# Convolution module of a two-layer trunk: GpSimd's additions moved to VectorE and TensorE

## The chip, the cores and the metric

The kernel runs on one core of a Trainium2 chip. The metric is the device time of one execution in microseconds (us). The engines are named as the profile names them: PE is TensorE (PEld its weight load), DVE is VectorE, ACT is ScalarE, POOL is GpSimd, SP is the engine whose queue issues most transfers.

## The reference, cut to what matters

Two layers run over 512 tokens of width 1024. Layer 0 is attention, layer 1 is the convolution module below, and each is followed by an expert mixer that takes most of the time. All of it is fp32.

```python
def conformer_conv(h, w_pw1, b_pw1, w_dw, b_dw, g_ln, b_ln, w_pw2, b_pw2):
    d = h.shape[-1]
    a = h @ w_pw1 + b_pw1
    a = a[..., :d] * jax.nn.sigmoid(a[..., d:])
    a = lax.conv_general_dilated(a, w_dw[:, None, :], ..., feature_group_count=d) + b_dw   # 31 taps per channel
    a = jax.nn.silu(layer_norm(a, g_ln, b_ln))
    return a @ w_pw2 + b_pw2

y_lat = conformer_conv(a_lat, *conv_p)
h_lat = h_lat + g1[:, None, :] * y_lat
```

## The kernel before

Channels lie on the 128 partitions, so the 1024 channels are eight blocks (f = 0 to 7), and the 512 tokens lie along the free axis. Nothing is scheduled by a planner here: every engine runs its instructions in the order in which `conv` issues them, and waits for a tile of another engine by semaphore.

An fp32 product is made of three matmuls on a high and a low half of each operand (`matmul3`, profile lines L142, L143, L144). The halves of a weight tile are made by `split`: ACT copies the high half (`cu_hi`, L1624), POOL subtracts it for the low half (`cu_lo`, L1625).

For every block `glu(f)` does two products of 24 matmuls each (`pw1`, weights `cu_raw` streamed by SP into two buffers, split two products ahead), a sigmoid on ACT (`sg`, L1664) and a multiplication on DVE that writes the padded block `pad` (L1668). Then the 31 taps of the block are run by one of four ways, by the letter in `CONV_BY = "vvgpvvmp"`:

- v: 31 instructions on DVE (`conv_dve`; L1680 and L1682 are its first two, L1684 all others, L1686 the sum of its two accumulators);
- g: ACT scales the shifted block (`tap`, L1698) and POOL adds it up (L1699), in `conv_pool`;
- m: 16 taps on DVE, 15 by ACT and POOL, added at L1779;
- p: on PE, 31 taps of three matmuls on diagonal matrices (`conv_pe`). The diagonals are built by one DVE instruction for the high half (`build_diag`, L1707) and 31 ACT instructions for the low half (L1710), and `split_pad` halves the block (L1717, L1718).

The lists `vq`, `gq` and `dq` hold the taps that are due, and `advance` issues so many of them after each `glu`. Then comes the layer norm: the mean by PE (`mu`, L1740), the subtraction (L1792), the variance by PE (`var`, L1795), a reciprocal square root on POOL, and per block a scaling on DVE (`xn`, L1815), a SiLU and a copy on ACT (`xs`, `sT`) and the low half of `sT` on DVE (L1823). Beside it POOL multiplies the last bias by the gate (L1803) and adds it to the residual `h` (L1805, four times).

The last product is a `RowProduct`: eight rows of weights `wo_raw` are loaded, multiplied by the gate on POOL (`prescale`, L1537) and split (`wo_hi` on ACT L1549, `wo_lo` L1550 on POOL for the first two rows and on DVE after that). `run` goes through the rows one after the other with 24 matmuls each (L1567), and adds the result to `h` at the end. `norm_transposed` ahead of all this transposes and modulates the input; its low halves (`caT`, L132) go to DVE and POOL in turn.

Of the kernel before, what the change touches and what calls it, by code (L numbers as in the profile page):

```python
# [25 lines left out]
T = 512  # L26
TT = 4
# [87 lines left out]
        return [self.out[tt] for tt in range(TT)]  # L115


def norm_transposed(k, work, ps, xr, A, sh, hi, lo, per_k=None):

    nc = k.nc  # L120
    nt = TT
    fs = {}
    for kk in range(KD + 2):
        if kk < KD:
            p = ps.tile([128, nt, 128], F32, name="nt_p", bufs=2)
            for tt in range(nt):
                nc.tensor.transpose(p[:, tt, :], xr[tt][:, kk * 128:(kk + 1) * 128], k.ident)
            f = work.tile([128, nt * 128], F32, name="nt_f", bufs=4)
            nc.scalar.activation(f, p.rearrange("p a b -> p (a b)"), AF.Identity, scale=A[:, kk:kk + 1],
                                 bias=sh[:, kk:kk + 1])  # L130
            nc.vector.tensor_copy(hi[:, kk, :], f)
            (nc.gpsimd if kk % 2 else nc.vector).tensor_tensor(lo[:, kk, :], f, hi[:, kk, :].bitcast(F32),  # L132
                                                               op=OP.subtract)
            fs[kk] = f
        if kk >= 2 and per_k is not None:
            per_k(kk - 2, fs.pop(kk - 2))
# [1384 lines left out]
class RowProduct:  # L1521

    BUFS = 3

    def __init__(self, k, raw_pool, src, scale):
        self.k, self.rp, self.src, self.scale, self.raw = k, raw_pool, src, scale, {}
        self.n = self.ns = 0

# [5 lines left out]

    def prescale(self):
        t = self.raw[self.ns]
        self.k.nc.gpsimd.tensor_tensor(t, t, self.scale, op=OP.mult)  # L1537
        self.ns += 1

    def split(self, j, eng=None):  # L1540
# [16 lines left out]
        for j in range(2):  # L1557
            self.split(j, eng)

    def run(self, lhs2, y, done):  # L1560
        nc = self.k.nc

        def mm(j, w2, tt):
            s = slice(tt * 128, (tt + 1) * 128)
            for n, (l, w) in enumerate(((lhs2[0], w2[0]), (lhs2[0], w2[1]), (lhs2[1], w2[0]))):
                for hf in range(2):
                    nc.tensor.matmul(y[tt][hf], lhsT=l[:, j, s], rhs=w[:, hf * 512:(hf + 1) * 512],  # L1567
                                     start=(j == 0 and n == 0), stop=(j == KD - 1 and n == 2))
        for j in range(KD - 2):
            for tt in range(TT):  # L1570
                mm(j, self.ws[j], tt)
            self.split(j + 2)
        for tt in range(TT):
            for j in (KD - 2, KD - 1):
                mm(j, self.ws[j], tt)
            done(tt)
# [2 lines left out]

CW = 31  # L1580
PADW = T + CW - 1
CONV_BY = "vvgpvvmp"
CONV_G = (6, 6, 6, 6, 6, 6, 6, 6)


def conv(k, a, h, xr, xp, hA, ada):
# [9 lines left out]
    owr = st.enter_context(k.pool("c_owr"))  # L1596
    proj = RowProduct(k, owr, lambda j: a["w_pw2"][j * 128:(j + 1) * 128, :], g1b)
    cv = cp.tile([128, KD, T], F32, name="cv")

    p1 = ExitStack()  # L1600
# [88 lines left out]
    def conv_pool(f, o, w0=0):

        pad = pads[f]
        if w0 == 0:
            S.activation(o, pad[:, 0:T], AF.Identity, scale=wdw[:, f, 0:1], bias=vec["b_dw"][:, f:f + 1])
        else:
            S.activation(o, pad[:, w0:w0 + T], AF.Copy, scale=wdw[:, f, w0:w0 + 1])
        for w in range(w0 + 1, CW):
            t = wk.tile([128, T], F32, name="tap", bufs=3)
            S.activation(t, pad[:, w:w + T], AF.Copy, scale=wdw[:, f, w:w + 1])  # L1698
            G.tensor_tensor(o, o, t, op=OP.add)  # L1699
            yield  # L1700

    diag = {}

    def build_diag(f, eng):

        d = diag[f] = [dg.tile([128, CW, 128], F32R, name="diag%d" % i) for i in range(2)]
        eng.tensor_tensor(d[0], k.ident[:, None, :].to_broadcast([128, CW, 128]),  # L1707
                          whi[:, f, :, None].bitcast(F32).to_broadcast([128, CW, 128]), op=OP.mult)
        for c in range(CW):
            S.activation(d[1][:, c, :], k.ident, AF.Copy, scale=wlo[:, f, c:c + 1])  # L1710
            yield

    def split_pad(f):
# [5 lines left out]
        return ph, pl  # L1719

    def conv_pe(f, ph, pl):
        p = ps.tile([128, T], F32, name="cz", bufs=4)
        dh, dl = diag.pop(f)
        for w in range(CW):
            matmul3(nc, p, (dh[:, w, :], dl[:, w, :]), (ph[:, w:w + T], pl[:, w:w + T]), w == 0, w == CW - 1)
        return lambda: S.activation(cv[:, f, :], p, AF.Identity, bias=vec["b_dw"][:, f:f + 1])
# [16 lines left out]
    vq, gq = [], []  # L1743
    dq = [build_diag(3, V)]
    part = wk.tile([128, T], F32, name="cv3")
    advance(dq, 8)
    for f in range(8):
        glu(f)
        by = CONV_BY[f]
        if by == "v":  # L1750
            vq.append(conv_dve(f))
        elif by == "g":
            gq.append(conv_pool(f, cv[:, f, :]))
        elif by == "m":
            vq.append(conv_dve(f, 16))
            gq.append(conv_pool(f, part, 16))
        if f == 3:
            pad_hl = split_pad(3)
        if f == 4:
            move = conv_pe(3, *pad_hl)  # L1760
        if f == 5:
            move()
            dq.append(build_diag(7, V))
            for j in range(proj.BUFS):
                proj.load()
        if f == 7:
            for g in (0, 1, 3, 2, 4):
                mean(g)
            move = conv_pe(7, *split_pad(7))
        advance(dq, 1000 if f == 6 else 12)  # L1770
        advance(vq, 26 if f == 4 else 14)
        if f == 7:
            for j in range(proj.BUFS):
                proj.prescale()
        advance(gq, CONV_G[f])
    while vq or gq:
        advance(vq, 2)
        advance(gq, 1)
    V.tensor_tensor(cv[:, 6, :], cv[:, 6, :], part, op=OP.add)  # L1779
    move()  # L1780
    us.close()
# [49 lines left out]
    def residual(tt):  # L1831
# [146 lines left out]
```

## Time and profile before

| | |
|---|---|
| median of 3 runs (lowest, highest) | 3433.71 us (3431.82, 3434.04) |
| the profiled execution: its time, its span | 3434.28 us, 3432.5 us |
| mean granted clock of PE | 0.968 |
| busy share of the span | PE 94%, PEld 81%, DVE 76%, ACT 38%, POOL 35% |
| the convolution module in the span | about 1836 to 2125 us |

The page of the profile cuts the span into 40 equal slices. The module is slices 22 to 25, which are the only ones after the start in which the PE row of tenths falls to 5 to 8, and in which the granted clock falls to 0.7 to 0.9. Times below are us from the start of the span.

### The profile page before, as it was taken

The page shows a single profiled execution, that of the slowest core. Times are in us where ns is not written, and L with a number is a line of the kernel's source. Part 1 is how long each engine was busy: PE and PEld are TensorE (multiplying, and loading weights), DVE is VectorE, ACT ScalarE, POOL GpSimd, SP SyncE. Part 2 cuts the span into 40 slices and gives each one's busy share as a digit, 9 for nine tenths or more (in the row PEclk, how much of TensorE's full clock was granted, in tenths as well). Part 3 has the DMA queues.
Part 4 walks back from the last instruction along what each step waited for, and adds up shares of the span by engine and source line. Part 5 has one row for each costly group of instructions (what it writes and reads, how often), then busy time and mean ns, then how long its engine had stood idle before and what let it go on. Part 6 is the DMA issues. An engine that isn't in the chain of part 4 may idle for free.

```text
span 3432.5 us, 46075 instructions
## 1 busy us (share of the span) xinstructions
PE 3228.5 (94%) x17044; PEld 2791.2 (81%) x17044; DVE 2604.2 (76%) x4765; ACT 1297.2 (38%) x2053; POOL 1189.0 (35%) x911
## 2 busy tenths in 40 slices
PE   8889999999999999999998757997899999999998
PEld 5766568889999999999876636887899999999986
DVE  3667646899577777777788985799777777777787
ACT  4325533344433333333334423234433333333332
POOL 1247533300133333333344844320023333333433
PEclk9989999999999999999999978998999999999999
DMA  6422224358788888889882102324788888888886
GB/s 201 153 72 72 85 99 155 105 202 294 264 301 307 303 308 303 303 302 310 312 303 88 56 13 94 121 99 183 254 284 302 304 305 311 297 308 301 305 318 213
DMA packets 373682, 764.36 MB, mean 223 GB/s; under 512 B 24144, under 2 KB 221008, under 8 KB 366160
## 3 DMA queue, kind: packets, MB, share of 16 engines
q1 hardware_dynamic: 292816, 442.62, 38.2%
q0 software_dynamic: 73728, 268.47, 22.8%
q10 hardware_dynamic: 6912, 50.33, 3.7%
q8 instruction: 133, 2.18, 0.3%
q14 instruction: 93, 0.76, 0.1%
HBM read 702.61 MB, written 58.72 MB: 222 GB/s over the span
## 4 chain that ended last, share of the span: by engine, by line
PE 73%; DVE 17%; DMA 3%; issue 3%; ACT 2%; POOL 1%; SPq 1%; ACTq 0%; DVEq 0%; POOLq 0%
PE acc L602 26%; PE s L142 11%; PE s L143 11%; PE s L144 11%; DVE cv L1684 4%; PE y L1567 2%; DVE eij L451 2%; PE ot L1352 1%; DVE al L454 1%; PE z L144 1%; DVE u_lo L173 1%; PE z L142 1%; PE z L143 1%; DVE ah L453 1%; PE scp L257 1%
## 5 line engine op out<-in xcount | busy, mean ns | idle before, releaser
L143 PE MATMUL s<-hhi,u_lo 128*128 128x384 f32 (+1 forms) x2304 | 792.8, 344 | 8.3 <-DVE u_lo L173 8.0
L142 PE MATMUL s<-hhi,u_hi 128*128 128x384 f32 (+1 forms) x2304 | 797.4, 346 | 3.0 <-ACT u_hi L169 3.0
L144 PE MATMUL s<-hlo,u_hi 128*128 128x384 f32 (+1 forms) x2304 | 791.3, 343 | 0.0
L613 POOL DMA_INDIRECT row<-in_u_dram,eidx x256 | 317.2, 1239 | 1019.3 <-DVE row L621 500.0
L613 POOL DMA_INDIRECT row<-in_v_dram,eidx x256 | 353.2, 1380 | 538.2 <-DVE gacc L625 480.1
L581 DVE TENSOR_TENSOR v_lo<-v_raw,v_hi 128x1024 fp32r<-128x1024 f32 x192 | 235.3, 1225 | 398.7 <-ACT v_hi L579 398.7
L579 ACT ACTIVATE v_hi<-v_raw 128x1024 fp32r<-128x1024 f32 x192 | 203.8, 1062 | 683.1 <-PE acc L602 646.5
L143 PEld LDWEIGHTS s<-hhi,u_lo 128*128 128x128 f32 x2304 | 436.7, 190 | 29.1 <-DVE u_lo L173 11.6
L142 PEld LDWEIGHTS s<-hhi,u_hi 128*128 128x128 f32 x2304 | 437.4, 190 | 20.0 <-ACT u_hi L169 3.7
L144 PEld LDWEIGHTS s<-hlo,u_hi 128*128 128x128 f32 x2304 | 436.4, 189 | 10.2
L602 PE MATMUL acc<-v_hi,w_hi 128*128 128x512 f32 x1344 | 418.1, 392 | 4.6 <-ACT w_hi L590 4.6
L602 PE MATMUL acc<-v_hi,w_lo 128*128 128x512 f32 x1344 | 416.3, 391 | 0.0
L602 PE MATMUL acc<-v_lo,w_hi 128*128 128x512 f32 x1344 | 416.1, 391 | 0.0
L173 DVE TENSOR_TENSOR u_lo<-u_raw,u_hi 128x1024 fp32r<-128x1024 f32 x242 | 295.0, 1219 | 45.4 <-ACT u_hi L169 45.0
L625 DVE SCALAR_TENSOR_TENSOR gacc<-row,gwgt,gacc 128x1024 f32<-128x1024 f32 x254 | 325.4, 1281 | 4.3
L169 ACT ACTIVATE u_hi<-u_raw 128x1024 fp32r<-128x1024 f32 x288 | 302.1, 1049 | 6.0 <-ACT stg L471 3.8
L621 DVE SCALAR_TENSOR_TENSOR row<-row,hg 128x1024 f32<-128x1024 f32 x256 | 300.9, 1219 | 0.0
L602 PEld LDWEIGHTS acc<-v_lo,w_hi 128*128 128x128 f32 x1344 | 252.4, 188 | 55.9
L602 PEld LDWEIGHTS acc<-v_hi,w_lo 128*128 128x128 f32 x1344 | 252.2, 188 | 54.6
L602 PEld LDWEIGHTS acc<-v_hi,w_hi 128*128 128x128 f32 x1344 | 249.1, 188 | 46.6 <-ACT w_hi L590 7.3
L590 ACT ACTIVATE w_hi<-w_f 128x384 fp32r<-128x384 f32 x256 | 134.7, 526 | 327.4 <-DVE w_f L588 306.8
L310 ACT ACTIVATE ring<-s 128x384 f32<-128x384 f32 x256 | 125.8, 491 | 323.8 <-PE s L144 323.7
(455 smaller groups left out, 5168.3 us busy)
## 6 DMA issues: line engine op xcount, KB each, us to landing
u_raw<-in_uT_dram SPq DMA_DIRECT2D x256, 512.0 KB
v_raw<-in_v_dram SPq DMA_DIRECT2D x192, 512.0 KB
Gd<-stg ACTq DMA_DIRECT2D x48, 1024.0 KB
g_in<-Gd SPq DMA_DIRECT2D x128, 384.0 KB
ada_w<-in_w_ada_dram SPq DMA_DIRECT2D x80, 512.0 KB
u_raw<-in_v_dram SPq DMA_DIRECT2D x64, 512.0 KB
u_raw<-in_wq_dram SPq DMA_DIRECT2D x32, 512.0 KB
ada_w<-in_w_ada_dram SPq DMA_DIRECT2D x8, 1024.0 KB
```

What stands on the lines that cost most here:

```text
L142: nc.tensor.matmul(out, lhsT=lh, rhs=rh, start=first, stop=False)
L143: nc.tensor.matmul(out, lhsT=ll, rhs=rh, start=False, stop=False)
L144: nc.tensor.matmul(out, lhsT=lh, rhs=rl, start=False, stop=last)
L169: nc.scalar.activation(uh, u, AF.Copy)
L173: lo_eng.tensor_tensor(ul, u, uh.bitcast(F32), op=OP.subtract)
L579: nc.scalar.activation(vh, v, AF.Copy)
L581: nc.vector.tensor_tensor(vl, v, vh.bitcast(F32), op=OP.subtract)
L602: nc.tensor.matmul(acc[tt][hf], lhsT=w[:, s], rhs=v[:, hf * 512:(hf + 1) * 512], start=f and n == 0, stop=l and n == 2)
L613: nc.gpsimd.indirect_dma_start(out=r, out_offset=None, in_=un if n < 128 else vn, in_offset=bass.IndirectOffsetOnAxis(ap=eidx[:, c:c + 1], ...
L621: nc.vector.scalar_tensor_tensor(r, r, 1.0, hg, op0=OP.mult, op1=OP.mult, accum_out=act[:, c:c + 1])
L625: nc.vector.scalar_tensor_tensor(gacc, r, wgt[:, c:c + 1], gacc, op0=OP.mult, op1=OP.add)
L1684: V.scalar_tensor_tensor(d, pad[:, w:w + T], wt, d, op0=OP.mult, op1=OP.add)
```

## The change

No arithmetic of the module is left on POOL but the reciprocal square roots of four numbers; it keeps the clearing of the 15 columns at both ends of `pad`.

- The low halves `cu_lo` and all of `caT` go to DVE.
- Blocks 0, 2, 4, 6 have all 31 taps on DVE; blocks 1, 3, 5 all 31 on PE; block 7 has 21 on PE and 10 on DVE, added at the end (before: DVE 0, 1, 4, 5; PE 3, 7; ACT with POOL block 2 and half of 6). A table `CONV_ORDER` sets the order: "p" is `glu` of a block, "c" the taps of a block on PE, and the last number says how many instructions of DVE's list follow.
- The low halves of the diagonals have one buffer (`diag_lo`), the high halves two; their ACT instructions are issued between the two products of `glu`.
- `RowProduct` gets an engine for `prescale` (DVE here, POOL as before in layer 0). Its pool opens in block 7, the first three rows are loaded there, and the first two are split before block 7's sum.
- The bias goes to `h` on DVE between the rows of the last product (`beside`).

```diff
-            (nc.gpsimd if kk % 2 else nc.vector).tensor_tensor(lo[:, kk, :], f, hi[:, kk, :].bitcast(F32),
+            (nc.gpsimd if kk % 2 and pool_odd else nc.vector).tensor_tensor(lo[:, kk, :], f, hi[:, kk, :].bitcast(F32),
...
-        self.k.nc.gpsimd.tensor_tensor(t, t, self.scale, op=OP.mult)
+        self.eng.tensor_tensor(t, t, self.scale, op=OP.mult)
...
             self.split(j + 2)
+            if beside is not None:
+                next(beside, None)
...
-CONV_BY = "vvgpvvmp"
+PE_TAPS = {1: CW, 3: CW, 5: CW, 7: 21}
+CONV_ORDER = (("p", 0, 0), ("p", 1, 8), ("p", 2, 10), ("c", 1, 23), ("p", 3, 8), ("p", 4, 10), ("c", 3, 23),
+              ("p", 5, 8), ("p", 6, 10), ("c", 5, 23), ("p", 7, 12), ("c", 7, 1000))
...
-        G.tensor_tensor(lo, u, hi.bitcast(F32), op=OP.subtract)
+        V.tensor_tensor(lo, u, hi.bitcast(F32), op=OP.subtract)
...
+    def diag_hi(f):
+        n = PE_TAPS[f]
+        dhi[f] = dg.tile([128, CW, 128], F32R, name="diag_hi", bufs=2)
+        V.tensor_tensor(dhi[f][:, 0:n], k.ident[:, None, :].to_broadcast([128, n, 128]),
+                        whi[:, f, 0:n, None].bitcast(F32).to_broadcast([128, n, 128]), op=OP.mult)
+
+    def diag_lo(f):
+        dlo[f] = dg.tile([128, CW, 128], F32R, name="diag_lo", bufs=1)
+        for c in range(PE_TAPS[f]):
+            S.activation(dlo[f][:, c, :], k.ident, AF.Copy, scale=wlo[:, f, c:c + 1])
             yield
...
+    for kind, f, n in CONV_ORDER:
+        if kind == "p":
+            glu(f, lambda: advance(lq, 8))
+            if f in PE_TAPS:
+                split_pad(f)
+            if PE_TAPS.get(f) != CW:
+                vq.append(conv_dve(f, PE_TAPS.get(f, 0)))
...
+            advance(vq, n)
+        else:
+            advance(lq, 1000)
+            if f == 7:
+                for g in range(5):
+                    mean(g)
+            p = conv_pe(f)
+            if f + 2 in PE_TAPS:
+                diag_hi(f + 2)
+                lq.append(diag_lo(f + 2))
+                advance(lq, 10)
+            if PE_TAPS[f] == CW:
+                S.activation(cv[:, f, :], p, AF.Identity, bias=vec["b_dw"][:, f:f + 1])
+            advance(vq, n)
+    proj.start(ow)
+    V.tensor_tensor(cv[:, 7, :], p, cv[:, 7, :], op=OP.add)
...
-    G.tensor_tensor(b2b, b2b, g1b, op=OP.mult)
-    for tt in range(TT):
-        G.tensor_tensor(h[:, tt, :], h[:, tt, :], b2b, op=OP.add)
...
+    def bias():
+        V.tensor_tensor(b2b, b2b, g1b, op=OP.mult)
+        yield
+        for tt in range(TT):
+            V.tensor_tensor(h[:, tt, :], h[:, tt, :], b2b, op=OP.add)
+            yield
+    proj.run(sT, y, residual, bias())
```

**POOL, from the taps to the end of the norm.** Before, low halves and additions of taps alternate on POOL (the first rows are those of block 3), and after the last additions it has weights, the norm's square root and the bias:

```order
L1625 TENSOR_TENSOR cu_lo<-cu_raw,cu_hi 128x1024 x2
L1666 MEMSET pad 128x15
L1667 MEMSET pad 128x15
L1699 TENSOR_TENSOR cv<-cv,tap 128x512 x6
...
L1550 TENSOR_TENSOR wo_lo<-wo_raw,wo_hi 128x1024 x2
L75 TENSOR_SCALAR lnr<-lnv 128x4
L76 TENSOR_TENSOR lnr<-lnr,neghalf 128x4
L1803 TENSOR_TENSOR b2b<-b2b,g1b 128x1024
L1805 TENSOR_TENSOR h_16342<-h_16342,b2b 128x1024 x4
```

Now eight pairs of clearing rows are followed at once by the square root and by that of the next norm:

```order
L1671 MEMSET pad 128x15
L1672 MEMSET pad 128x15
L75 TENSOR_SCALAR lnr<-lnv 128x4
L76 TENSOR_TENSOR lnr<-lnr,neghalf 128x4
L75 TENSOR_SCALAR nt_r<-nt_ss 128x1
```

Every instruction on a large tile has left POOL's queue here.

**DVE, from block 2 to block 3.** DVE now does the low halves itself. This is its queue from the end of block 2's `glu` (`pad`) to the low halves of the weights of block 4; 10 taps stand ahead of `diag_hi`, 23 behind it:

```order
L1627 TENSOR_TENSOR cu_lo<-cu_raw,cu_hi 128x1024 x2
L1673 SCALAR_TENSOR_TENSOR pad<-cz,vec_16435,sg 128x64x8
L1689 SCALAR_TENSOR_TENSOR cv<-pad,vec_16435,cv 128x512
...
L1700 TENSOR_TENSOR diag_hi<-ident,whi 128x3968
L1689 SCALAR_TENSOR_TENSOR cv<-pad,vec_16435,cv 128x512
...
L1627 TENSOR_TENSOR cu_lo<-cu_raw,cu_hi 128x1024 x2
L1673 SCALAR_TENSOR_TENSOR pad<-cz,vec_16435,sg 128x64x8
L1713 CAST pad_hi<-pad 128x542
L1714 TENSOR_TENSOR pad_lo<-pad,pad_hi 128x542
```

The low halves that PE needs two products later stand behind all 33 taps and the diagonals.

**DVE, the end of the taps.** Before, the two sums were followed at once by the subtraction of the mean:

```order
L1686 TENSOR_TENSOR cv<-cv,cv_17616 128x512
L1779 TENSOR_TENSOR cv<-cv,cv_16558 128x512
L1792 TENSOR_TENSOR cv<-cv,mu 128x512 x8
L1798 TENSOR_TENSOR lnd<-var,ident 128x512
```

Now the scaling of three rows and the low halves of two rows of the last product's weights stand between the last tap and block 7's sum:

```order
L1691 TENSOR_TENSOR cv<-cv,cv_17660 128x512
L1538 TENSOR_TENSOR wo_raw<-wo_raw,g1b 128x1024 x2
L1551 TENSOR_TENSOR wo_lo<-wo_raw,wo_hi 128x1024
L1538 TENSOR_TENSOR wo_raw<-wo_raw,g1b 128x1024
L1551 TENSOR_TENSOR wo_lo<-wo_raw,wo_hi 128x1024
L1772 TENSOR_TENSOR cv<-cz,cv 128x512
L1780 TENSOR_TENSOR cv<-cv,mu 128x512 x8
```

Five instructions on 128x1024 tiles have come from POOL to this place.

## Rows read from the trace of the kernel before

**Rows 1.** Windows: from:to, length, busy PE, PEld, DVE, ACT, POOL, granted clock, DMA.

```profile
1852.30:2041.60 189.30, 142.35 (x561) 110.29 (x559) 185.22 (x159) 72.17 (x134) 121.55 (x78) 0.86 0.13 42
2041.60:2065.60 24.00, 13.97 (x20) 5.00 (x20) 11.72 (x12) 6.72 (x11) 11.04 (x7) 0.67 0.14 44
2065.60:2089.70 24.10, 14.91 (x48) 11.26 (x48) 22.14 (x16) 13.01 (x19) 14.07 (x6) 0.71 0.00 0
2089.70:2125.20 35.50, 35.42 (x146) 28.47 (x146) 13.23 (x15) 8.51 (x11) 10.04 (x9) 0.94 0.21 75
```

**Rows 2.** The chain of waits, 1836 to 2126 us, shares by line.

```profile
by line: DVE cv L1684 44.0%; PE y L1567 12.1%; issue 5.2%; DVE xn L1815 4.2%; POOL cv L1699 3.5%; PE var L1795 3.4%; POOL cu_lo L1625 2.5%; DVE sT L1823 2.5%; DVE pad L1668 2.2%; DVE caT L132 1.9%; ACT cu_hi L1624 1.7%; DVE diag L1707 1.5%;
```

**Rows 3.** Groups by line, 1700 to 2100 us: busy us, mean ns of one.

```profile
L1684 DVE SCALAR_TENSOR_TENSOR cv<-pad,vec,cv 128x512 f32<-128x512 f32 x130 | 152.8, 1247 | 0.0
...
L1710 ACT ACTIVATE diag<-ident,wlo 128x128 fp32r<-128x128 f32 x62 | 18.7, 392 | 3.6 <-DVE wlo L1645 3.6
```

**Rows 4.** Windows, DVE's taps of L1684 alone: length, busy us (count), granted clock, DMA.

```profile
1946.40:1966.50 20.10, 20.10 (x14) 0.92 0.08 26
...
2019.50:2040.90 21.40, 19.79 (x30) 1.00 0.00 0
```

**Rows 5.** The same two windows, all of POOL: length, busy us (count), granted clock, DMA.

```profile
1946.40:1966.50 20.10, 17.21 (x12) 0.92 0.08 26
...
2019.50:2040.90 21.40, 0.00 (x0) 1.00 0.00 0
```

**Rows 6.** Timeline of DVE: start us, length us, instructions merged.

```profile
1836.26 0.75 DVE L110 TENSOR_SCALAR nt_x<-h,nt_r 128x1024 f32<-128x1024 f32 x1 [1.57 <-ACT cu_hi L1624]
1851.68 4.28 DVE L1707 TENSOR_TENSOR diag<-ident,whi 128x3968 fp32r<-128x3968 f32 x1
2013.27 1.09 DVE L1668 SCALAR_TENSOR_TENSOR pad<-cz,vec,sg 128x512 f32<-128x512 f32 x1
2014.46 0.45 DVE L1717 CAST pad_hi<-pad 128x542 fp32r<-128x542 f32 x1
2046.43 4.87 DVE L1792 TENSOR_TENSOR cv<-cv,mu 128x512 f32<-128x512 f32 x8 [2.17 <-PE mu L1740]
2060.61 2.83 DVE L1806 TENSOR_TENSOR lnd<-ident,lnr 128x512 f32<-128x512 f32 x1 [1.50 <-POOL lnr L76]
2065.60 1.09 DVE L1815 TENSOR_TENSOR xn<-cv,mu 128x512 f32<-128x512 f32 x1 [2.17 <-PE mu L1809]
2071.48 3.27 DVE L1815 TENSOR_TENSOR xn<-cv,lnrs 128x512 f32<-128x512 f32 x1
2089.72 3.50 DVE L1550 TENSOR_TENSOR wo_lo<-wo_raw,wo_hi 128x1024 fp32r<-128x1024 f32 x3 [0.25 <-ACT wo_hi L1549]
```

**Rows 7.** Timeline of PE, same columns; the bracket is the wait ahead.

```profile
1852.33 0.39 PE L142 MATMUL cz<-caT,cu_hi 128*128 128x512 f32 x1
1857.77 0.39 PE L142 MATMUL cz<-caT,cu_hi 128*128 128x512 f32 x1
...
1915.03 0.39 PE L142 MATMUL cz<-pad_hi,diag 128*128 128x512 f32 x1
...
1936.66 0.40 PE L142 MATMUL cz<-caT,cu_hi 128*128 128x512 f32 x1
...
1980.84 3.59 PE L1740 MATMUL mu<-cv,onesd 128*128 128x512 f32 x8
2015.06 0.77 PE L142 MATMUL cz<-pad_hi,diag 128*128 128x512 f32 x1 [19.38 <-DVE pad_hi L1717]
2047.84 9.83 PE L1795 MATMUL var<-sq,onesd 128*128 128x512 f32 x16 [1.44 <-ACT sq L1794]
2068.73 1.22 PE L1567 MATMUL y<-wo_hi,sT 128*128 128x512 f32 x2 [3.17 <-ACT sT L1821]
2089.74 1.22 PE L1567 MATMUL y<-wo_hi,sT 128*128 128x512 f32 x2 [5.29 <-ACT wo_hi L1549]
2124.38 0.62 PE L1567 MATMUL y<-wo_hi,sT 128*128 128x512 f32 x2
```

More of the change, by code (lines that the diff above doesn't have):

```diff
@@ L115, in finish, with norm_transposed @@
         return [self.out[tt] for tt in range(TT)]
-def norm_transposed(k, work, ps, xr, A, sh, hi, lo, per_k=None):
+def norm_transposed(k, work, ps, xr, A, sh, hi, lo, per_k=None, pool_odd=True):
     nc = k.nc
@@ L1523, with __init__ @@
     BUFS = 3
-    def __init__(self, k, raw_pool, src, scale):
+    def __init__(self, k, raw_pool, src, scale, eng=None):
+        self.eng = eng or k.nc.gpsimd
         self.k, self.rp, self.src, self.scale, self.raw = k, raw_pool, src, scale, {}
@@ L1558, in start, with run @@
             self.split(j, eng)
-    def run(self, lhs2, y, done):
+    def run(self, lhs2, y, done, beside=None):
         nc = self.k.nc
@@ L1581 @@
 PADW = T + CW - 1
-CONV_BY = "vvgpvvmp"
-CONV_G = (6, 6, 6, 6, 6, 6, 6, 6)
+PE_TAPS = {1: CW, 3: CW, 5: CW, 7: 21}
+CONV_ORDER = (("p", 0, 0), ("p", 1, 8), ("p", 2, 10), ("c", 1, 23), ("p", 3, 8), ("p", 4, 10), ("c", 3, 23),
+              ("p", 5, 8), ("p", 6, 10), ("c", 5, 23), ("p", 7, 12), ("c", 7, 1000))
 def conv(k, a, h, xr, xp, hA, ada):
@@ L1595, in conv @@
     b2b = hA.tile([128, D], F32, name="b2b")
-    owr = st.enter_context(k.pool("c_owr"))
-    proj = RowProduct(k, owr, lambda j: a["w_pw2"][j * 128:(j + 1) * 128, :], g1b)
     cv = cp.tile([128, KD, T], F32, name="cv")
@@ L1634, in conv @@
         tile = staticmethod(lambda shape, dt, name, bufs=2: ps.tile(shape, dt, name="cz", bufs=4))
-    norm_transposed(k, W, PP, xr, A, ada.par, aT[0], aT[1])
+    norm_transposed(k, W, PP, xr, A, ada.par, aT[0], aT[1], pool_odd=False)
     ns.close()
@@ L1659, in conv, with glu @@
     pads = {}
-    def glu(f):
-        z2, z1 = pw1(2 * f), pw1(2 * f + 1)
+    def glu(f, between):
+        z2 = pw1(2 * f)
+        between()
+        z1 = pw1(2 * f + 1)
+        between()
         sg = wk.tile([128, T], F32, name="sg", bufs=2)
         S.activation(sg, z2, AF.Sigmoid, bias=vec["b_pw1"][:, 8 + f:9 + f])
-        pad = wk.tile([128, PADW], F32, name="pad", bufs=5)
+        pad = wk.tile([128, PADW], F32, name="pad", bufs=4)
         G.memset(pad[:, 0:15], 0.0)
@@ L1671, in glu, with conv_dve @@
         pads[f] = pad
-    def conv_dve(f, n=CW):
+    def conv_dve(f, w0=0):
         pad = pads[f]
         o = (cv[:, f, :], wk.tile([128, T], F32, name="cv2", bufs=2))
-        for w in range(n):
+        for w in range(w0, CW):
             d, wt = o[w % 2], wdw[:, f, w:w + 1]
-            if w == 0:
-                V.tensor_scalar(d, pad[:, 0:T], wt, vec["b_dw"][:, f:f + 1], op0=OP.mult, op1=OP.add)
-            elif w == 1:
+            if w == w0:
+                V.tensor_scalar(d, pad[:, w:w + T], wt, vec["b_dw"][:, f:f + 1], op0=OP.mult, op1=OP.add)
+            elif w == w0 + 1:
                 V.tensor_scalar(d, pad[:, w:w + T], wt, None, op0=OP.mult)
@@ L1687, in conv_dve @@
         yield
[L1689 to L1710, printed above, removed]
+    dhi, dlo, halves = {}, {}, {}
+    def diag_hi(f):
[7 more added lines that the diff above has]
+            S.activation(dlo[f][:, c, :], k.ident, AF.Copy, scale=wlo[:, f, c:c + 1])
             yield
@@ L1718, in split_pad, with conv_pe @@
         V.tensor_tensor(pl, pad, ph.bitcast(F32), op=OP.subtract)
-        return ph, pl
-    def conv_pe(f, ph, pl):
+        halves[f] = ph, pl
+    def conv_pe(f):
         p = ps.tile([128, T], F32, name="cz", bufs=4)
[L1723 to L1726, printed above, removed]
+        (ph, pl), dh, dl, n = halves.pop(f), dhi.pop(f), dlo.pop(f), PE_TAPS[f]
+        for w in range(n):
+            matmul3(nc, p, (dh[:, w, :], dl[:, w, :]), (ph[:, w:w + T], pl[:, w:w + T]), w == 0, w == n - 1)
+        return p
     def advance(gens, n):
@@ L1741, in mean @@
         sums[0] += 1
[L1743 to L1781, printed above, removed]
+    vq, lq = [], [diag_lo(1)]
+    for kind, f, n in CONV_ORDER:
[5 more added lines that the diff above has]
+                vq.append(conv_dve(f, PE_TAPS.get(f, 0)))
+            if f == 0:
+                diag_hi(1)
+            if f == 7:
+                us.close()
+                owr = sp.enter_context(k.pool("c_owr", side="right"))
+                proj = RowProduct(k, owr, lambda j: a["w_pw2"][j * 128:(j + 1) * 128, :], g1b, V)
+                for j in range(proj.BUFS):
+                    proj.load()
+                sT_pool = sp.enter_context(k.pool("c_sT", side="right"))
+                ow = sp.enter_context(k.pool("c_o", side="right"))
+            advance(vq, n)
+        else:
+            advance(lq, 1000)
+            if f == 7:
+                for g in range(5):
[8 more added lines that the diff above has]
+            advance(vq, n)
@@ L1782, in conv @@
+    proj.start(ow)
+    V.tensor_tensor(cv[:, 7, :], p, cv[:, 7, :], op=OP.add)
     ds.close()
     lp = p1.enter_context(k.pool("c_l"))
-    sT_pool = sp.enter_context(k.pool("c_sT", side="right"))
     sT = [sT_pool.tile([128, KD, T], F32R, name="sT%d" % i) for i in range(2)]
-    ow = sp.enter_context(k.pool("c_o", side="right"))
-    proj.start(ow, G)
-    for f in (5, 7, 6):
+    for f in (5, 6, 7):
         mean(f)
@@ L1835, in residual @@
         nr.add(tt, h[:, tt, :])
-    proj.run(sT, y, residual)
+    def bias():
[5 more added lines that the diff above has]
+    proj.run(sT, y, residual, bias())
     p3.close()
```

## The prediction

> **What bounds the kernel now.** I first cut the module into stretches [rows 1]. In the long one, 189.3 us of taps, DVE is busy 185.2 us and PE 142.4 at a mean granted clock of 0.86. The chain of waits says the same: 44.0% of the module hangs on DVE's taps, no other line over 12.1% [rows 2]. So a tap is the thing to price. Its mean is 1247 ns over 130 [rows 3], but that mean hides two kinds. In one window 14 taps fill 20.10 us while POOL is busy 17.21; in another 30 taps take 19.79 us, 0.66 each, with POOL at 0.00 [rows 4, 5]. Fourteen at 0.66 are 9.2 us, so half of the first window is not the taps' own work. The slow taps stand where POOL works. PE meanwhile waits for DVE, 19.38 us ahead of block 7's taps [rows 7].
>
> **The start.** DVE's last row scaling ends at 1837.0 [rows 6]. Now two low halves of weights follow. A 128x1024 subtraction costs 1.17 us (three in 3.50, POOL idle, ACT at work beside them [rows 6]): 1839.4. Then come eight pairs of cast and subtraction, about 1.05 each (a 128x512 subtraction is 4.87/8 = 0.61, a cast of 542 columns 0.45 [rows 6]): 1847.8. PE's first product can end some 1.2 us behind, near 1849.0, where it ended at 1852.33 [rows 7]: **-3.3 us**. Bounds: 0 if the grant stays at the lower level for longer, -3.5.
>
> **The taps, on PE.** A product of 24 matmuls takes 1857.77 - 1852.33 = 5.44 us, a block of 93 tap matmuls 1936.66 - 1915.03 = 21.63, that is 0.233 each, and a block's mean two matmuls of 3.59/8 = 0.45 [rows 7]. After the first product PE has 15 products (81.6), three full tap blocks (64.9), five means (4.5) and 63 tap matmuls of block 7 (14.65): 165.65 us, to 2014.65 if it never waits. The Trainium skill, page TensorE: Matmul & The Clock Gate, section "Wait — 56ns, not 53.3ns?", puts back-to-back matmuls of 512 columns 215.7 ns apart at 2.4 GHz; an estimate by it gives the 702 matmuls 151.4 us instead of 161.2. This case's rows show 227 and 233, the latter pitch also in block 7's taps at a grant of 1.00 [rows 4], so the trace does not agree, and the measurement decides.
>
> **Does DVE keep up?** One round is two blocks' `glu` and one tap block: PE 4 x 5.44 + 21.63 = 43.4 us. DVE has four low halves (4.7), two `pad` at 1.0 to 1.09 (2.1), a `split_pad` (0.45 and about 0.7), one `diag_hi` (4.28 [rows 6]) and 41 taps (27.1): 39.3. So PE sets the round, with 4 us to spare. Two places are tighter:
> - The low halves behind the 33 taps. When PE starts a tap block, DVE has `pad` (1.0), 10 taps (6.6), `diag_hi` (4.3) and 23 taps (15.2): 27.1 us, then the subtraction, 28.3. PE wants it after its tap block and two products that are split already, 21.6 + 10.9 = 32.5. Spare: 4.2 us.
> - The end. PE's last product ends at 1995.5. DVE then has `pad`, `split_pad`, 14 taps, two sums and five operations on weights, 1.0 + 1.15 + 9.2 + 1.2 + 5.9 = 18.5: 2014.0, just ahead of PE's 2014.65.
>
> ACT, 72 us busy of 189 [rows 1], loses 44 scalings and gains 52 diagonals at 18.7/62 = 0.30 us [rows 3]. Because the low diagonals have one buffer, ACT waits for PE's tap block to end, and behind it the weights' high halves; ten diagonals (3.0), the bias copy (under 1) and a high half (as long as its subtraction, 1.2) make that 5.2 us after the tap block, against 5.5 (27.1 - 21.6) at which DVE asks and 10.9 at which PE asks. I take no wait. The first three rows of `wo_raw` are loaded behind the last of `cu_raw`, tens of us before use; POOL's clearings run as soon as a buffer is free.
>
> After 2014.65 PE does two more means (1.8), which cover block 7's sum on DVE (0.6), and the last mean (0.9): the first subtraction is at 2017.4, before at 2046.43 [rows 6]. **-29.0 us**, the start's 3.3 included.
>
> **The norm.** From there to the first `xn` it took 2065.60 - 2046.43 = 19.2 us. `lnd` at 2.83 us should fall to about 0.7, since POOL no longer adds the bias beside it: **-2.1**. The variance took 9.83 us for 16 matmuls; at 0.45 they are 7.2, with PE coming from work. Half of that: **-1.3** (bounds 0 and -2.6). First `xn` near 2033.2.
>
> **The last product.** Before, PE started 3.1 us after the first `xn`, stopped for the third row's weights 5.29 us and went on 24.1 us after it; the last two matmuls, from 2124.38, end near 2124.8, 59.2 after it [rows 7]. One `xn` is 3.27 us and the first 1.09 [rows 6]: DVE waited for POOL's bias and weights, 14.1 us of work in 24.1 [rows 1]. Now eight pairs of `xn` and subtraction (1.09 + 0.61) are over 13.6 us after the start of the first, with ACT's SiLU and copy behind the last `xn` about 15; the third row's high half is there at 16.2, its scaling and low half on DVE by 17.8. PE reaches that row at 18.2: 3.1 and the 15.7 that the first two rows took (2089.74 - 5.29 - 2068.73), less some 0.6 of waits for `sT` in them. The other 144 matmuls at 0.2267 take 32.6: 50.8 instead of 59.2, **-8.4**. DVE then owes each row 3.5 us (scaling, low half, bias) within 5.44.
>
> **Sum.** -29.0 - 2.1 - 1.3 - 8.4 = -40.8 us. The profiled execution took 3434.28 (span 3432.5): 3393.5. The median of the runs is 0.6 below the profiled one, so I predict **3393 us**. The rest of the program is issued in the same order, and its first loads wait for nothing later than the last bias, some 15 us ahead of the product's end.
>
> **The rivals.**
> - *DVE stays the bound.* DVE takes over POOL's subtractions, so if a tap does not hold 0.66 the round turns to DVE: at 43.4 - 12.2 = 31.2 us for 41 taps, 0.76 each. The midpoint between 0.66 and the mean pitch 152.8/130 = 1.175 [rows 3] is about 0.90: 49.1 a round, 5.7 over, three times, and 14 taps at the end 3.4: +20, **3413**. For it: the margin is 10%. Against it: 30 taps in a row at 0.66 with PE busy. Chance 0.12.
> - *The last product waits for its weights.* The third row's low half is needed two matmuls after 18.2 and comes at 17.8. If DVE is late there or PE falls back to the lower grant, the 8.4 us are lost: **3402**. Chance 0.12.
> - *Slower: POOL was not what slowed DVE.* If long taps come from something else that stays (PE, ACT or transfers), moving work to DVE only adds to it. 124 taps at 1.175 (145.7), ten first taps and five sums (9.7), pads (8.4), twelve low halves (14.0), splits (4.6), diagonals (15.8), weights (5.9): 204 us from the first `pad` near 1856 (the second product's end at 1854.4 and a sigmoid), so 2060, with the means 2063 against 2046.43, and the tail gains nothing: 3434 + 16 = **3450**. It decides from a pitch of about 1.04. The Trainium skill's Perfetto Trace Analysis, section Optimizing Scalar/DVE Operations, speaks for the old split: with DVE saturated, give work to ACT or even GpSimd; it adds that those two share a read port and that it might not help. Against it stands the zero of POOL beside the fast taps, and the three subtractions of 3.50 us beside a busy ACT. Chance 0.04.
> - *It does not do what it says*, the gain being taken back by the next layer's first loads: 3434. The stages behind wait for the module's last row, so 0.02.
>
> **Numbers.** The forecast has 0.70; its own range is 3386 (both bounds, and the product's first rows at the full grant) to 3400. For 8 in 10 I go from 3386 to 3412, which leaves out the slower case, no change and the outer part of the DVE case. Measurement of this kernel tells about 0.2%, 6.9 us, from no change. Faster: 0.70 + 0.12 + 0.12 = 0.94; same 0.02; slower 0.04.
>
> **What would show it.** Right: taps of 0.66 pitch throughout, POOL nearly idle from 1836 on, PE's taps stretch with a grant near 1.00 and waits of under 2 us in all, the first subtraction near 2017, no stop inside the last product. Wrong: PE waiting for `cu_lo` after a tap block (DVE the bound), PE waiting for `wo_lo` (the product), taps over 1 us with POOL idle (the slower case). The sum fails most easily at the two tight places on DVE.

## The result and the profile after

The changed kernel takes **3389.44 us** (median of 4 runs, 3388.94 to 3395.2); before it was 3432.77 on the same chip. The ratio is **0.9875, 95% interval 0.9863 to 0.9887**: 43.3 us less. The profile is of the 3395.2 us execution (span 3392.9), which was late before the module began: the last row scaling, DVE's `nt_x`, starts at 1839.21, before at 1836.26 [rows 6]. So the stretches below are measured from that instruction. (On the page of the kernel before, PE's row falls to 7 and 8 tenths in slices 28 and 29 as well; they lie behind the module.)

Windows of the changed kernel, columns as in [rows 1]: the taps, the norm, the last product's first two rows of weights, its other six rows.

```profile
1851.50:2017.00 165.50, 165.50 (x713) 133.85 (x713) 140.91 (x179) 56.68 (x141) 0.88 (x8) 1.00 0.16 51
2017.00:2034.00 17.00, 11.83 (x25) 4.29 (x23) 7.63 (x13) 6.46 (x10) 1.21 (x2) 0.94 0.11 37
2034.00:2051.60 17.60, 13.99 (x51) 11.05 (x51) 15.70 (x19) 13.96 (x19) 0.00 (x0) 0.77 0.00 0
2051.60:2085.20 33.60, 32.72 (x144) 26.83 (x144) 22.39 (x25) 7.70 (x10) 2.21 (x6) 1.00 0.26 81
```

The roles are exchanged. PE is busy for all 165.50 us of the taps, at a grant of 1.00; DVE is busy 140.91 and POOL 0.88. The chain of waits of the changed kernel, 1836 to 2085 us, by line:

```profile
by line: PE cz L144 22.4%; PE cz L142 22.4%; PE cz L143 22.3%; PE y L1568 13.0%; DVE xn L1800 3.0%; PE var L1783 2.9%; PE mu L1736 2.8%; PE cz L127 2.2%; DVE sT L1808 1.7%; PE mu L1794 0.8%; issue 0.8%; ACT xs L1805 0.6%; POOL h L643 0.6%; 
```

Where DVE's taps held 44.0% [rows 2], PE's products and taps (`cz`) hold 67% now, and DVE's taps are no longer among these lines. The groups by line, 1839 to 2020 us, show what a tap costs:

```profile
L1689 DVE SCALAR_TENSOR_TENSOR cv<-pad,vec,cv 128x512 f32<-128x512 f32 x124 | 83.2, 742 | 0.0
...
L1627 DVE TENSOR_TENSOR cu_lo<-cu_raw,cu_hi 128x1024 fp32r<-128x1024 f32 x16 | 19.1, 1217 | 5.2 <-ACT cu_hi L1626 5.2
```

A tap took 1247 ns in the mean before [rows 3], 742 now, at a pitch of 83.2/124 = 0.67 us. DVE's timeline of the changed kernel, at the places of [rows 6], with the `pad` of blocks 2, 4 and 6:

```profile
1839.21 0.89 DVE L110 TENSOR_SCALAR nt_x<-h,nt_r 128x1024 f32<-128x1024 f32 x1 [1.58 <-ACT cu_hi L1626]
1878.83 1.14 DVE L1673 SCALAR_TENSOR_TENSOR pad<-cz,vec,sg 128x512 f32<-128x512 f32 x1 [1.34 <-PE cz L144]
1922.26 1.15 DVE L1673 SCALAR_TENSOR_TENSOR pad<-cz,vec,sg 128x512 f32<-128x512 f32 x1 [0.84 <-PE cz L144]
1965.68 1.15 DVE L1673 SCALAR_TENSOR_TENSOR pad<-cz,vec,sg 128x512 f32<-128x512 f32 x1 [0.84 <-PE cz L144]
1998.23 1.10 DVE L1673 SCALAR_TENSOR_TENSOR pad<-cz,vec,sg 128x512 f32<-128x512 f32 x1 [7.17 <-PE cz L144]
2017.08 0.69 DVE L1772 TENSOR_TENSOR cv<-cz,cv 128x512 f32<-128x512 f32 x1 [0.38 <-PE cz L144]
2019.66 4.87 DVE L1780 TENSOR_TENSOR cv<-cv,mu 128x512 f32<-128x512 f32 x8 [1.88 <-PE mu L1736]
2031.14 0.69 DVE L1791 TENSOR_TENSOR lnd<-ident,lnr 128x512 f32<-128x512 f32 x1 [1.49 <-POOL lnr L76]
2034.00 1.07 DVE L1800 TENSOR_TENSOR xn<-cv,mu 128x512 f32<-128x512 f32 x1 [2.17 <-PE mu L1794]
```

Now DVE waits for PE (7.17 us ahead of the last `pad`), and ahead of block 7's sum both come within 0.38 us. PE's timeline, answering to [rows 7], from the start of the second product on:

```profile
1851.34 0.39 PE L142 MATMUL cz<-caT,cu_hi 128*128 128x512 f32 x1
2021.06 7.13 PE L1783 MATMUL var<-sq,onesd 128*128 128x512 f32 x16 [1.44 <-ACT sq L1782]
2037.12 1.22 PE L1568 MATMUL y<-wo_hi,sT 128*128 128x512 f32 x2 [3.16 <-ACT sT L1806]
2051.57 0.74 PE L1568 MATMUL y<-wo_lo,sT 128*128 128x512 f32 x2 [0.49 <-DVE wo_lo L1551]
```

The eight additions of `y` to `h` at the module's end, before and now (the last two numbers ahead of the shapes are the starts of the first and the last):

```profile
L1834 DVE TENSOR_TENSOR h<-y,h x8: 679/686/692, 2116.6 to 2125.4; 128x512 f32<-128x512 f32 x8
```

```profile
L1819 DVE TENSOR_TENSOR h<-y,h x8: 678/686/692, 2075.7 to 2084.5; 128x512 f32<-128x512 f32 x8
```

From the last row scaling to the first subtraction of the mean: 2046.43 - 1836.26 = 210.2 before, 2019.66 - 1839.21 = 180.5 now, **-29.7**. From there to the first `xn`: 19.2 before, 14.3 now, **-4.8**. From the first `xn` to the last of those additions: 59.8 and 50.5, **-9.3**. The module gains 43.8.

### The profile page after: what moved, and what is told of

Read it like the earlier page. It is cut to its first block, busy times and chain, and to the rows that moved or that the text cites. A ratio compares the mean times of both kernels' runs of the same rounds, so it can differ in the third digit from the quotient of the medians.

```text
span 3392.9 us, 46305 instructions
## 1 busy us (share of the span) xinstructions
PE 3249.8 (96%) x17200; PEld 2815.6 (83%) x17200; DVE 2555.0 (75%) x4800; ACT 1282.3 (38%) x2060; POOL 1025.5 (30%) x832
## 4 chain that ended last, share of the span: by engine, by line
PE 79%; DVE 12%; DMA 3%; issue 2%; ACT 2%; SPq 1%; POOL 0%; ACTq 0%; DVEq 0%; POOLq 0%
PE acc L602 26%; PE s L143 11%; PE s L142 11%; PE s L144 11%; PE y L1568 2%; DVE eij L451 2%; PE cz L144 2%; PE cz L142 2%; PE cz L143 2%; PE ot L1352 1%; DVE al L454 1%; PE z L144 1%; DVE u_lo L173 1%; PE z L142 1%; PE z L143 1%
```

## The experiments

The theory: GpSimd instructions that read SBUF hold up VectorE's taps; with them gone a tap costs 0.67 us and TensorE bounds the taps. The main rival: the gain is that of more taps on TensorE and of the new order.

**Three dummy loads on GpSimd.** Into the changed kernel, behind each block's clearing of `pad`, one of three lines (`sc` is scratch):

```
         pads[f] = pad
+        for _ in range(6):
+            G.tensor_tensor(sc[2], sc[0], sc[1], op=OP.add)   # e1_adds
+            G.memset(sc, 0.0)                                 # e2_memsets, 128x1536
+            G.tensor_copy(sc[2], sc[0])                       # e3_copies
```

> The changed kernel, with six additions of two 128x512 scratch tiles on GpSimd behind each block's clearing of pad (48 in all; nothing reads their result). Theory (GpSimd instructions that read SBUF hold up VectorE's two-input instructions): in before, 14 taps lost 10.9 us while POOL was busy 17.2, some 0.63 us for each us of POOL; 48 additions at before's 1.67 us are 80 us of POOL, so VectorE loses about 50 us, of which its idle 27 us between 1852 and 2020 take a part: first subtraction 20 to 45 us later, 3410 to 3435, taps beside the additions at a pitch of 1.1 or more. Rival (the taps were long for another reason, and the gain is that of the new order and of more taps on PE): taps stay at 0.67, 3389.

> The same places, but 48 clearings of a 128x1536 scratch tile on GpSimd, which read nothing. Theory (reading is what holds VectorE up): taps stay at 0.67 beside them, 3389 (to 3392). Rival (any busy GpSimd holds VectorE up, reading or not): the loss per us of POOL as in the run with additions, +15 us or more. POOL's busy time is to be of the same order as with the additions.

> The same places, but 48 copies of a 128x512 scratch tile on GpSimd, one input each. Theory, wide form (any GpSimd instruction that reads SBUF excludes a two-input VectorE instruction for its whole length): the loss for each us of POOL is as with the additions, so 3400 to 3430 as the copies' time has it. Narrow form (only a GpSimd instruction with two inputs does it): 3389. Rival (something else made taps long): 3389 here and with the additions.

Measured: additions **3428.41** us, clearings **3394.44**, copies **3400.1** (the kernel before 3434.38 on that chip, 1.6 above its median above). One place serves for all four kernels: the eight taps behind the second `pad_lo` (that of block 3). DVE's timeline there, in the changed kernel,

```profile
1913.76 5.39 DVE L1689 SCALAR_TENSOR_TENSOR cv<-pad,vec,cv 128x512 f32<-128x512 f32 x8
```

with the additions (and, from the module's start, one of the eight casts of the transposed input),

```profile
1841.53 1.49 DVE L131 CAST caT<-nt_f 128x512 fp32r<-128x512 f32 x1
...
1937.89 11.61 DVE L1694 SCALAR_TENSOR_TENSOR cv<-pad,vec,cv 128x512 f32<-128x512 f32 x8
```

with the clearings,

```profile
1839.76 0.69 DVE L132 TENSOR_TENSOR caT<-nt_f,caT 128x512 fp32r<-128x512 f32 x1
1840.37 0.96 DVE L131 CAST caT<-nt_f 128x512 fp32r<-128x512 f32 x1
...
1913.16 5.38 DVE L1692 SCALAR_TENSOR_TENSOR cv<-pad,vec,cv 128x512 f32<-128x512 f32 x8
```

and with the copies:

```profile
1919.48 7.50 DVE L1694 SCALAR_TENSOR_TENSOR cv<-pad,vec,cv 128x512 f32<-128x512 f32 x8
```

POOL's timeline beside them, first with the additions, then with the clearings, then with the copies (and one copy, of an earlier group of six, that ran while VectorE stood idle, with VectorE's next instruction):

```profile
1938.14 10.15 POOL L1681 TENSOR_TENSOR sc<-sc,sc 128x512 f32<-128x512 f32 x6
```

```profile
1913.40 8.60 POOL L1679 MEMSET sc<- 128x1536 f32 x6
```

```profile
1919.72 6.07 POOL L1681 COPY sc<-sc 128x512 f32<-128x512 f32 x6
```

```profile
1860.17 0.61 POOL L1681 COPY sc<-sc 128x512 f32<-128x512 f32 x1
1861.56 1.23 DVE L1627 TENSOR_TENSOR cu_lo<-cu_raw,cu_hi 128x1024 fp32r<-128x1024 f32 x1 [1.93 <-ACT cu_hi L1626]
```

The same eight taps take 5.39 us beside an idle POOL, 5.38 beside 8.6 us of clearings, 7.50 beside six copies and 11.61 beside six additions. So an addition costs the taps (11.61 - 5.39)/6 = 1.04 us, a copy 0.35, a clearing nothing. For a tap a busy POOL isn't what matters; what POOL reads is. Neither form that was expected for the copies holds: they do cost the taps something, against the narrow form, and a tap does not pay in proportion to POOL's time, as the wide form had it, since a copy costs a third of an addition in 60% of its time. The hold is mutual: a copy takes 0.61 us beside an idle VectorE and about 1.0 beside the taps. With the additions the first subtraction comes 217.2 us after the last row scaling, 36.8 later than in the changed kernel: some 16 at the start, where the casts and subtractions take 24.8 instead of 8.6 us, the rest in the taps and the low halves. So 48 additions that nobody needs give back most of the gain. The 5 us of the clearings, 2 more than was expected, are of another kind, and all at the start: the eight casts take 0.95 to 1.00 us beside them (the first 0.77) instead of 0.42, some 4.1 us together, and the last row scaling 1.93 instead of 0.89, while the subtractions between the casts stay at 0.69.

**The kernel before without GpSimd's additions.** The other way round: the old order, with one line removed.

```
             S.activation(t, pad[:, w:w + T], AF.Copy, scale=wdw[:, f, w:w + 1])
-            G.tensor_tensor(o, o, t, op=OP.add)
```

> The kernel before with GpSimd's 44 additions of taps left out (blocks 2 and 6 are then incomplete); its order, its taps on VectorE and TensorE and GpSimd's low halves stay. Theory: the 130 taps lose the hold of 44 additions of 1.67 us, 73.6 us of POOL at 0.63, about 46 us, and TensorE's order gives the next bound: 3390 to 3410, mean of a tap from 1.25 to about 0.9. Rival (the gain came from moving taps to TensorE and from the new order): 3425 to 3433, mean of a tap as before.

Measured: **3390.48** us, 43.9 less than before, with the taps' order and their split between VectorE and TensorE as before. The groups by line, 1836 to 2060 us, first DVE's, then POOL's:

```profile
L1684 DVE SCALAR_TENSOR_TENSOR cv<-pad,vec,cv 128x512 f32<-128x512 f32 x130 | 111.9, 934 | 0.0
```

```profile
L1625 POOL TENSOR_TENSOR cu_lo<-cu_raw,cu_hi 128x1024 fp32r<-128x1024 f32 x16 | 44.8, 2813 | 64.5 <-ACT cu_hi L1624 64.4
```

The same 130 taps take 111.9 instead of 152.8 us [rows 3]; what they still have over 0.67 each (87 us) stands beside the low halves and the scalings of the last product's weights that POOL kept. ScalarE's 44 scalings of taps still run here, so it was not they that held VectorE. The first subtraction comes 172.9 us after the last row scaling, where it came 210.2 before and 180.5 in the changed kernel. That settles the main rival: without the new order and without more taps on TensorE the taps get as fast. What those two do there is the work of the additions, without POOL. That the whole time is the same as the changed kernel's is a coincidence of its parts: the norm takes 16.5 us here (19.2 before, 14.3 changed), and the product 60.2 (59.8 and 50.5), so the gain at the end of the module is not that of the additions.

**One part alone: the low halves.** In the kernel before, `cu_lo` on VectorE; in the changed kernel, `cu_lo` back on GpSimd.

```
-        G.tensor_tensor(lo, u, hi.bitcast(F32), op=OP.subtract)   # e5_before_lo, from before
+        V.tensor_tensor(lo, u, hi.bitcast(F32), op=OP.subtract)
-        V.tensor_tensor(lo, u, hi.bitcast(F32), op=OP.subtract)   # e6_lo_pool, from the change
+        G.tensor_tensor(lo, u, hi.bitcast(F32), op=OP.subtract)
```

> The kernel before with one part of the change alone: the 16 low halves cu_lo on VectorE, GpSimd's additions of taps stay. Theory: VectorE gets 16 subtractions of 1.22 us (19.5) and is rid of their hold. The run without additions still had taps of 0.934 us beside these 16, 0.19 more than the changed kernel's 0.742, over 130 taps 25 us; so -5 us, between -12 and +5: 3422 to 3438. Rival (GpSimd does not hold VectorE up): +14 to +20, 3447 to 3453.

> The changed kernel with one part undone: cu_lo back on GpSimd. Theory: VectorE loses some 25 us by the hold and gains 19 us of its own work, and in the taps it has 27 us idle behind TensorE, so the taps stay bound by TensorE and only the start, where two of them stand beside the casts of the transposed input, gets 2 to 4 us longer: 3390 to 3395. Rival (each such hold comes out in the time wherever it stands): 25 us, 3405 to 3415. Second rival (the low halves on VectorE were a cost that the change paid): under 3386.

Measured: in the old kernel **3427.91** us, ratio 0.9985 (0.9975 to 0.9994), 5 to 6 us better; in the new one **3397.28**, some 7 us worse than the changed kernel and 2 above the range expected. Sixteen subtractions, 22.1 us in all (1.42 each, beside POOL's additions), put on the very engine that bound the kernel made it a little faster: the 130 taps fell from 152.8 to 126.2 us, so VectorE was rid of a larger hold. In the changed kernel the taps' mean rises to 827 ns with `cu_lo` on POOL, and PE waits for nothing in the taps: the loss there lies in VectorE's idle time, as expected. The 5.8 us by which the first subtraction is late (186.2 instead of 180.5) come from the start, more than the 2 to 4 expected. DVE's timeline there, and PE's:

```profile
1836.13 2.32 DVE L848 SCALAR_TENSOR_TENSOR cvA<-ada_par,vec 128x8 f32<-128x8 f32 x1
...
1848.05 2.58 DVE L131 CAST caT<-nt_f 128x512 fp32r<-128x512 f32 x1
```

```profile
1850.69 0.50 PE L142 MATMUL cz<-caT,cu_hi 128*128 128x512 f32 x1 [1.83 <-DVE caT L131]
...
1852.77 0.63 PE L142 MATMUL cz<-caT,cu_hi 128*128 128x512 f32 x1
1853.19 0.63 PE L143 MATMUL cz<-caT,cu_lo 128*128 128x512 f32 x1
```

An 8-column operation takes 2.32 us (0.15 in the changed kernel), the last cast 2.58 instead of 0.42, PE stops 1.83 us for it, and then runs matmuls 0.42 us apart instead of 0.23. That is its granted clock, in windows of PE's stop and of what follows:

```profile
1848.90:1852.30 3.40, 1.61 (x5) 1.04 (x6) 3.13 (x5) 0.17 (x1) 1.45 (x1) 0.96 0.22 61
1852.30:1855.30 3.00, 3.00 (x8) 2.30 (x7) 0.00 (x0) 3.00 (x9) 0.00 (x0) 0.50 0.29 108
1855.40:1858.00 2.60, 2.60 (x13) 2.14 (x12) 0.00 (x0) 2.58 (x10) 2.40 (x3) 0.99 0.00 0
```

The grant behind the stop is 0.50, the 1.2 GHz level, and then 0.99 again. That was left out of the expectation.

**The tail undone.**

```
-                proj = RowProduct(k, owr, ..., g1b, V)
+                proj = RowProduct(k, owr, ..., g1b)
-    proj.start(ow)
+    proj.start(ow, G)
     (and V to G in bias())
```

> The changed kernel with the tail undone: scaling of the last product's weights, their first two low halves and the bias additions back on GpSimd; the order and the rest stay. Theory: the norm's lnd and xn are held again and the product waits for weights: lnd +2.1, the product +5 to +9: 3396 to 3401. Rival (the tail's gain came from the new order of means and the early loads): 3388 to 3391.

Measured: **3395.92** us, as expected in sum but not in its parts. The first `lnd` product is held again (2.82 us, +2.1). The product itself, from the first `xn` (2034.89) to the last addition of `y` (2086.7), takes 51.8 us: only 1.3 more than in the changed kernel, not 5 to 9. That POOL is free of the taps is not the reason: in the kernel before without additions it is free of theirs too, and there the product takes 60.2 us (from 2026.34 to 2086.5). What differs is POOL's work beside the eight `xn`. POOL's timeline there, and PE's stop:

```profile
2023.70 10.81 POOL L1804 TENSOR_TENSOR h<-h,b2b 128x1024 f32<-128x1024 f32 x4
2034.48 5.93 POOL L1537 TENSOR_TENSOR wo_raw<-wo_raw,g1b 128x1024 f32<-128x1024 f32 x2
```

```profile
2050.41 1.22 PE L1567 MATMUL y<-wo_hi,sT 128*128 128x512 f32 x2 [6.38 <-ACT wo_hi L1549]
```

And POOL's with the tail undone:

```profile
2034.88 2.36 POOL L1538 TENSOR_TENSOR wo_raw<-wo_raw,g1b 128x1024 f32<-128x1024 f32 x1
2037.20 3.09 POOL L1825 TENSOR_TENSOR h<-h,b2b 128x1024 f32<-128x1024 f32 x1
```

In the old order POOL works 14.1 us behind the first `xn`; in the new one, with the bias between the rows, 5.4 us, and PE does not stop for the third row. So most of the product's gain is the new order's. Which part of that order does it, the place of the bias or the early loads, no run separates.

The rest, 4.2 us, is ahead of the norm. DVE's timeline at block 7's pad, and PE's:

```profile
1994.62 2.32 DVE L1713 CAST pad_hi<-pad 128x542 fp32r<-128x542 f32 x1
1996.97 2.76 DVE L1714 TENSOR_TENSOR pad_lo<-pad,pad_hi 128x542 fp32r<-128x542 f32 x1
```

```profile
1999.79 0.50 PE L144 MATMUL cz<-pad_lo,diag_hi 128*128 128x512 f32 x1 [1.75 <-DVE pad_lo L1714]
...
2002.18 0.63 PE L143 MATMUL cz<-pad_hi,diag_lo 128*128 128x512 f32 x1
```

POOL's work on the weights now falls on the two operations that TensorE waits for, 0.44 and 0.72 us long otherwise, and the stop is again followed by matmuls 0.43 us apart, at a grant of 0.50 from 2001.3 to 2004.4.

**Versions that give TensorE less.** If TensorE is the bound, taps moved to VectorE pay. Blocks 1, 3 and 5 get a second part on VectorE, which is added to TensorE's sum; ScalarE makes the high diagonals.

```
-PE_TAPS = {1: CW, 3: CW, 5: CW, 7: 21}
+PE_TAPS = {1: 27, 3: 27, 5: 27, 7: 17}      # e8; e9: 7: 16; e10: 25, 25, 25, 16
+            S.activation(dhi[f][:, c, :], k.ident, AF.Copy, scale=whi[:, f, c:c + 1].bitcast(F32))
+                vq.insert(0, conv_dve(f, PE_TAPS[f]))
+            V.tensor_tensor(cv[:, g, :], q, cv[:, g, :], op=OP.add)
```

> A version that gives TensorE less: blocks 1, 3 and 5 with 27 taps on TensorE and 4 on VectorE, block 7 with 17 and 14, five more of block 6's taps ahead of block 7's pad, and the high diagonals of blocks 3, 5 and 7 made by ScalarE (31 scalings of the identity's columns instead of one VectorE product). Theory (TensorE's 165.7 us bind the taps, 0.70 us a tap, VectorE has slack): 16 taps less are -11.2 us, 3376 to 3383. Rival (VectorE is bound as well, it has no room for 16 taps more): 3386 to 3395. The chain of waits is to name TensorE's taps less and VectorE's more than in the changed kernel.

> The balanced version again, with VectorE's idle time ahead of the pads filled (28 instead of 23 taps handed out behind each tap block of TensorE, 11 or 12 instead of 10 ahead of it, and all of block 6 ahead of block 7's pad), 16 of block 7's taps on TensorE, and the last product's first weights scaled and split behind the eight subtractions of the mean, not ahead of the sum of block 7. Theory (in the first balanced version TensorE was freed 11.3 us early and waited for VectorE's last taps and weights, 28 us in one piece behind the last pad, while VectorE had stood idle some 20 us ahead of the pads): the first subtraction comes 9 to 12 us earlier than in the changed kernel, the weights give 2 us back in the norm: 3380 to 3384. Rival (VectorE's idle time can't be filled, since the pads wait for TensorE whatever is ahead of them): 3389 to 3395.

> As the second balanced version, but with 25 taps of blocks 1, 3 and 5 on TensorE and 6 on VectorE. Theory by TensorE: six taps less are another -4.2 us: 3376 to 3380. Rival (VectorE is full by then, 25 us of taps more than in the changed kernel against 27 us idle and 12.8 us of diagonals given away): no faster than the second balanced version, with TensorE waiting for VectorE ahead of the last means by 3 us or more.

> The changed kernel itself, on the same chip as the two balanced versions, so that a few us can be told apart: 3388 to 3393.

The first version missed: **3395.9** us, ratio 0.9889 (0.9872 to 0.9905), no gain over the change. Waits of PE in it, 1835 to 2020 us:

```profile
PE mu L1742 <- DVE cv L1790: 11.3, 1, 11.3
```

TensorE was done 11.3 us early, as 16 taps at 0.70 should be, and waited all of it for VectorE, which had stood idle ahead of the pads and then had 28 us in one piece behind the last one. The second version fills that idle time and moves the weights: **3384.92** us. The third takes six more taps from TensorE: **3379.99**, ratio 0.9835 (0.9817 to 0.9852). The changed kernel gave 3390.6 on that chip, 0.9864 (0.9848 to 0.9881). So the two are 5.7 and 10.6 us faster than the change, less than TensorE's taps alone would say. One reason is the norm, which takes 16.8 us (first subtraction to first `xn`) instead of 13.4. The weights behind the subtractions are 2.4 of these 3.4 us, where a gain of 2 had been expected; the other 1 us is a slower last pair of mean matmuls, which the changed kernel had too in its profile above. The other reason is the last step: the first subtraction comes 180.8 us after the last row scaling in the changed kernel on that chip, 168.5 in the second version and 166.7 in the third, so the last six taps brought 1.8 us, not 4.2. The medians of the second and third differ by 4.9 us, but their runs overlap (3381.89 to 3387.1 and 3378.65 to 3385.32), and the profiles show 1.9 of it in the module. The third version's window over the taps, and its waits of PE there:

```profile
1855.00:2004.00 149.00, 147.19 (x628) 117.58 (x627) 138.57 (x199) 61.07 (x167) 0.63 (x8) 1.00 0.15 50
```

```profile
PE cz L143 <- DVE cu_lo L1627: 1.8, 2, 1.2
```

VectorE is busy 93% of it and TensorE 99%, and TensorE now waits a little for VectorE's low halves: the two engines are nearly even, and there is little more to be had by moving taps.

## Why the prediction was right, step by step

The forecast was 3393 us, the median is 3389.4. The steps:

- **A tap costs 0.66 us once POOL is quiet.** Right: 0.67 over 124 taps. The runs with dummies show the cause and not only the coincidence that the two windows of [rows 4, 5] gave.
- **PE's walk of 165.65 us without a wait.** Right: 165.5 us at a grant of 1.00, and the first subtraction 29.7 us earlier where 29.0 was said. At the tight end of DVE's queue the forecast had 0.65 us of room, and the wait of 0.38 us is what was left of it. The rounds came as said, too: the `pad` of blocks 2, 4 and 6 start 43.4 us apart, and DVE is idle 4.3 us in each of the two rounds between them. Most of the rest of its 24.6 idle us, which the forecast did not work out, lies ahead of them (7.7) and ahead of block 7's `pad` (7.17).
- **The start, -3.3.** The second product starts 12.1 us after the last row scaling instead of 16.1: -3.9, a little beyond the bound of -3.5.
- **The norm.** `lnd` fell by 2.1 as said. The variance was mis-sized: half of 2.6 was taken, and it fell from 9.83 to 7.13, all of it. The norm's window has a mean grant of 0.94, where it had 0.67 [rows 1].
- **The last product, -8.4.** It fell by 9.3, with a stop of 0.49 us for the third row's low half. The reason, that POOL's bias and weights no longer stand beside the `xn`, is borne out, but VectorE's taking them over is the small part of it. With the same work on POOL in the new order the product still fell from 59.8 to 51.8 us: 8.0 of the 9.3 are the order's and 1.3 come from VectorE doing the work.
- **The sum.** -40.8 was said for the module, -43.8 was measured; the variance is 1.4 of the difference, the product 0.9, the start 0.6 and the taps 0.1. All four miss the same way, so nothing cancelled.
- **The rivals.** VectorE as the bound at 0.76 a tap did not come, nor the last product's wait. "POOL was not what slowed DVE" is refuted by the kernel before without additions. (The two engines that share a read port, in the sentence cited there, are VectorE and GpSimd.) That the gain comes from TensorE's larger share was no rival of the forecast and should have been one; the same run refutes it.

## What to carry to other kernels

Before an engine is called full, look whether its instructions have one length or two, and what the other engines do beside the long ones. Work given to GpSimd to relieve VectorE can cost VectorE more than doing it: an addition of 128x512 cost 1.04 us of taps in the run with dummies, where a tap itself takes 0.67, and sixteen subtractions of 128x1024 brought back to VectorE at 1.42 us each were a small gain even while VectorE was the bound. Once the bound has moved, the next gain needs both the share and the place: 16 taps less on TensorE were worth nothing until VectorE's idle time ahead of the pads was filled. And where two runs give the same total, compare their parts before you say that they do the same.

## What the hardware showed

The hold depends on what either side does. Taps, which have two inputs in SBUF, kept 0.67 us beside clearings, and lost 0.35 us to a copy and 1.04 us to an addition on POOL; the start's subtractions, with two inputs as well, stayed at 0.69 beside clearings and took 0.98 beside copies and 1.64 beside additions. Casts, with one input, took 0.96 instead of 0.42 us beside clearings, 0.83 beside copies and 1.49 beside additions. The length of VectorE's instruction doesn't protect it: one of 8 columns took 2.32 us, not 0.15, beside a subtraction of 128x1024 on POOL. The Trainium skill, SBUF — State Buffer, section "Who interferes with whom", says that a VectorE instruction with two SBUF inputs contends with a GpSimd instruction that reads SBUF and not with one that only writes, and that casts can enter a two-port mode that contends with GpSimd; these rows agree on both. Of that mode it also says that whoever issues first holds the shared ports for the whole instruction; no run here settles this, since a cast can come upon a clearing that is half done.

A short stop of TensorE costs more than itself: behind stops of 1.83 and 1.75 us the matmuls ran 0.43 us apart instead of 0.23, at a grant of 0.50 for some 3 us, and seven of them lost about 0.2 us each. In the changed kernel's taps, where TensorE makes no such stop, the grant is 1.00 throughout.
